# A transformer block with seven-product matmuls: wider weight tiles, x and early h parked in DRAM, and more seven-product chunks

## The chip, the cores and the metric

The kernel runs on one core of one Trainium2 chip. The time is device microseconds of one launch, the median over several runs. The engines in the text are TensorE (PE, with its weight loads as PEld), VectorE (DVE), ScalarE (ACT), GpSimd (POOL) and the queue engine SyncE (SP).

## The reference

One layer on x of 256 x 2048 in float32, batch 1:

```
h    = rms_norm(x, norm_mix);  proj = h @ w_in            # 2048 -> 11264 columns
q_a, f_a, i_a, g_a, q_b, k_b, v_b, gate_logits = split(proj)
gate_a, gate_b = split(sigmoid(gate_logits + b_gate))
y_a  = hgrn2_mixer(q_a, f_a, i_a, g_a)                    # 8 heads of 128, recurrence in chunks
y_b  = chunked_relpos_attention(q_b, k_b, v_b)            # 8 heads of 128
x   += (gate_a * (y_a @ w_proj_a) + gate_b * (y_b @ w_proj_b)) @ w_out
h    = rms_norm(x, norm_ffn)
gate, up = split(h @ w_ffn_in)                            # 2 x 5632 columns
x   += (silu(gate) * up) @ w_ffn_out                      # 5632 -> 2048
```

## The kernel before, in words

All products have 256 rows (two blocks of 128, m = 0 and 1). Weights are cut on the host into blocks of 512 columns and chunks of four k-tiles of 128 rows; one chunk of one block is 1 MB. Each weight is brought by DMA into `raw`, cast to a float32r high half `whi` by ScalarE, and the remainder `wlo` is subtracted out by VectorE. Each product of a 128x128 piece of the activation with a 128x512 piece of a weight is three matmuls, high x high, high x low, low x high (lines 168 to 170, and 222 to 224 in `triple`). Activations are held the same way, as pairs of high and low tiles.

`product` (line 153) computes one block of 512 columns into two PSUM banks: per chunk 4 k-tiles x 2 row blocks x 3 = 24 matmuls. `product_pair` (line 205) computes two blocks at once. In a plain chunk that is 48 matmuls. In a chunk that is listed in `forms`, the first two k-tiles of the chunk, the two row blocks and the two column blocks are treated as a 2 x 2 times 2 x 2 product and done with seven products where eight stand otherwise (`seven`, line 229). That needs four sums of weight tiles (`weight_forms`, line 188) and four sums of activation tiles (`act_forms`, line 318, kept as high and low halves), and eight PSUM banks: four that collect results (`cb`) and four for the shared terms (`ub`), which an epilogue adds up on VectorE after the last such chunk. The other two k-tiles (the "rest" of the chunk) stay plain. With `plain_first`, chunk 0 does its rest first.

The stages in order are: 22 blocks of w_in (with the recurrence and attention woven between the matmuls by generators, which `tick` advances every few products), of which the gate blocks nb = 1 and 3 are pairs in seven form; w_pa and w_pb with the gates; w_out (one pair in seven form, two single blocks); 11 SwiGLU pairs j (the gate block j and the up block 11 + j of w_fi; in seven form for j in `SEVEN_IN`, else two calls of `product`); and w_fo, two pairs of column blocks over 11 chunks, where chunk j reads the 512 columns of h that SwiGLU pair j made; chunks in `SEVEN` are in seven form. The activation forms for these are made when h is transposed (`transpose_split`, line 307, also a generator) and written to DRAM (`kept`), then all read back before w_fo.

Instructions are traced in program order and a planner orders them by priority and by when their inputs and buffers come free in its own model; weight preparation has a priority 500 instructions ahead of its place (`PREP_AHEAD`). An instruction that waits holds up what is behind it on its engine or queue. Raw weight tiles come on SP's queue; `x2_kept`, `kept`, `xt2`, `sf` and `x2` go on POOL's. Tiles come from pools of a fixed number of buffers: `raw` 8 of two 512-column blocks, `whi` and `wlo` 4 of two blocks each, `big` 33 tiles of 4 KB a partition for almost all activations, and two PSUM pools of four banks, `mm` and `aux`.

Of the kernel before, what the change touches and what calls it, by code (L numbers as in the profile page):

```python
# [10 lines left out]
F32 = mybir.dt.float32  # L11
# [6 lines left out]
P = 128  # L18
T = 256
# [17 lines left out]
SEVEN = (1, 2, 3, 5, 6, 7, 9)  # L37


SEVEN_IN = (1, 3, 5, 7, 9)  # L40
# [5 lines left out]
def block_kernel(ctx: ExitStack, tc: tile.TileContext, x, x_t, w_in, w_pa, w_pb, w_out, w_fi, w_fo,  # L46
# [77 lines left out]
    def fetch(w, nb, kc, n=2, pinned=False):  # L124

        res = []
        for hf in range(2):
            raw = wraw_p.tile([P, 2, 512], F32, tag="raw", name=nm("raw"))
            for k in range(0, 2, n):
                d = nc.sync.dma_start(out=raw[:, k:k + n, :],  # L130
                                      in_=w[nb, kc, :, 2 * hf + k:2 * hf + k + n, :])
                if pinned:
                    tc.keep_in_program_order(d)
            res.append(raw)
        return res

    def load_weights(w, nb, kc, n=2, raw=None):

        raw = fetch(w, nb, kc) if raw is None else raw
        res = []  # L140
        for hf in range(2):
            src = raw[hf]
            hi = whi_p.tile([P, 2, 512], F32R, tag="hi", name=nm("whi"))
            lo = wlo_p.tile([P, 2, 512], F32R, tag="lo", name=nm("wlo"))
            for k in range(0, 2, n):
                sl = slice(k, k + n)
                nc.scalar.copy(hi[:, sl, :], src[:, sl, :])  # L147
                nc.vector.tensor_tensor(out=lo[:, sl, :], in0=src[:, sl, :],  # L148
                                        in1=hi[:, sl, :].bitcast(F32), op=ALU.subtract)
            res += [(hi[:, 0, :], lo[:, 0, :]), (hi[:, 1, :], lo[:, 1, :])]  # L150
        return res

    def product(w, nb, n_chunks, act, prologue=None, last=False):

        ps = [mm.tile([P, 512], F32, tag="mm", name=nm("mm")) for _ in range(2)]
        for kc in range(n_chunks):
            if prologue is not None:
                ws = load_weights(w, nb, kc, 1 if kc < 2 else 2, prologue(kc))
            else:
                with tc.high_priority(offset=min(PREP_AHEAD, tc.cur_priority - first_block[0])):  # L160
                    ws = load_weights(w, nb, kc)
# [12 lines left out]
        return ps  # L174
# [5 lines left out]
    def halves(src):  # L180

        n = src.shape[1]
        hi = whi_p.tile([P, 2, 512], F32R, tag="hi", name=nm("whi"))
        lo = wlo_p.tile([P, 2, 512], F32R, tag="lo", name=nm("wlo"))
        split(hi[:, 0:n, :], lo[:, 0:n, :], src)
        return [(hi[:, k, :], lo[:, k, :]) for k in range(n)]

    def weight_forms(r0, r1):


        ta = t6_p.tile([P, 2, 512], F32, tag="t6", name=nm("ta"))
# [12 lines left out]

    def product_pair(w, nbs, n_chunks, act, forms, c_pool, u_pool, epilogue, plain_first=False,
                     last=False):
# [3 lines left out]
        tag = {id(mm): "mm", id(aux): "bank"}  # L210
        cb, ub = {}, {}
        count = [0]
# [16 lines left out]
        def seven(kc, tf):  # L229
            sf = forms[kc]  # L230
            form = {5: 0, 6: 1, 7: 2, 3: 3}
            plain = {1: (0, 0), 2: (1, 0), 4: (1, 1)}
            dest = {2: (0, 0), 3: (0, 1), 4: (1, 0)}
            for p in (1, 2, 3, 5, 7, 6, 4):
                if p in form:
                    a = (sf[:, 0, form[p], :], sf[:, 1, form[p], :])
                else:
                    k, m = plain[p]
                    a = act(kc * 4 + k, m)
                if p in dest:  # L240
                    triple(bank_of(cb, dest[p], c_pool), a, tf[p], False)
                else:
                    triple(bank_of(ub, p, u_pool), a, tf[p], kc == max(forms))
            if kc == max(forms):
                epilogue(ub)

        for kc in range(n_chunks):
            end = kc == n_chunks - 1
            early = plain_first and kc == 0
            with tc.high_priority(offset=min(PREP_AHEAD, tc.cur_priority - first_block[0])):  # L250
                r = [fetch(w, nb, kc) for nb in nbs]
                ws = [[None] * 4 for _ in nbs]
                if kc not in forms:
                    for n in range(2):
                        ws[n][0:2] = halves(r[n][0])
                        ws[n][2:4] = halves(r[n][1])
                else:
                    if not early:
                        tf = weight_forms(r[0][0], r[1][0])
                    for n in range(2):  # L260
                        ws[n][2:4] = halves(r[n][1])
                    if early:
                        tf = weight_forms(r[0][0], r[1][0])
            if kc in forms and not early:
                seven(kc, tf)
# [6 lines left out]
            if kc in forms and early:  # L272
                seven(kc, tf)
# [65 lines left out]

    def picker(tiles):  # L340
# [24 lines left out]
    def x_block(c):  # L365

        xt = t4([P, 4, T], "xt")
        with tc.high_priority():
# [6 lines left out]
            raw = fetch(w_in, 2, c, 1 if c < 2 else 2, pinned=True)  # L375
# [8 lines left out]
        if c == 3:  # L384
            with tc.high_priority():
                for i in range(4):
                    xn = t4([P, 2, 512], "x")
# [367 lines left out]
    def x_forms():  # L755

        for c in range(4):
            xt = t4([P, 2, T], "xt2")
            nc.gpsimd.dma_start(out=xt, in_=x_t[c, :, 0:2, :])
            fq[c] = t4([P, 2, 4, P], "fq", F32R)  # L760
            yield 1
            yield 1
            act_forms(xt, fq[c], par[:, C_NM + 4 * c:C_NM + 4 * c + 4])
# [37 lines left out]
    for nb in range(4):  # L801
# [63 lines left out]
    def swiglu_pair(j):  # L865
# [3 lines left out]
        def sums(ub):  # L869
# [3 lines left out]
        cb = product_pair(w_fi, (j, NJ + j), 4, act_x2, fx, aux, mm, sums, plain_first=True,  # L873
                          last=True)
# [7 lines left out]

    for j in range(NJ):
        if j in SEVEN_IN:
            hn = swiglu_pair(j)
        else:
            ps = product(w_fi, j, 4, act_x2)
# [3 lines left out]
            ps = product(w_fi, NJ + j, 4, act_x2)  # L891
# [7 lines left out]
        soon = dict(wait=0, pool=mm) if j + 1 in SEVEN_IN else {}  # L899
        start(transpose_split(hn, *hT[j], forms=f, spill=spill, **soon))  # L900
# [3 lines left out]
    forms = {}  # L904
    for j in SEVEN:
        forms[j] = t4([P, 2, 4, P], "sf", F32R)
        nc.gpsimd.dma_start(out=forms[j].bitcast(F32), in_=kept[j])
    for pair in range(2):
        nbs = (2 * pair, 2 * pair + 1)
        xs = {nb: t4([P, 2, 512], "x2") for nb in nbs}  # L910
        for nb in nbs:
            nc.gpsimd.dma_start(out=xs[nb], in_=x2_kept[nb])
        x0, x1 = (xs[nb] for nb in nbs)

        pools = (mm, aux) if pair == 0 else (aux, mm)
        cb = product_pair(w_fo, nbs, NJ, act_h, forms, *pools,
                          residual_sums(x0, x1), last=pair == 1)
# [72 lines left out]
```

## Time and profile before

| | us |
|---|---|
| median of 3 runs (lowest, highest) | 1428.51 (1427.79, 1428.94) |
| the profiled execution | 1427.22 |
| its span in the trace | 1425.4 |
| HBM read / written | 279.34 MB / 7.86 MB |

The trace holds one execution. A row of the timeline has the start, the length and the engine of an instruction, its line, its tiles as out<-in, the number of merged instructions, and in brackets how long the engine was idle before it and what ended that. Reported lengths of matmuls overlap their successors, so that what one costs is read from the distance of starts. In a row of a table of stretches, each engine's busy time is followed by its count of instructions; the last three figures are the granted clock of TensorE as a share of full speed, the busy share of the 16 DMA engines, and GB/s.

### The profile page before, as it was taken

Reading aid. Unit: us, or ns where it says so; the run is one execution under the profiler, and the core shown is the slowest. Engines: PE = TensorE matmul, PEld = TensorE weight load, DVE = VectorE, ACT = ScalarE, POOL = GpSimd, SP = SyncE. Lnnn points to the kernel's source line nnn. Section 1 sums busy time; section 2 is a strip of 40 time slices with the busy share of each in tenths; the row PEclk is TensorE's granted clock in tenths of the full one; section 3 lists DMA queues with packets and bytes.
Section 4 is the critical chain, followed back from the end, with each engine's and each line's share of the span. In section 5 each row is a group of like instructions: output and inputs, shape, how many; then the busy total and the mean of one; then the engine's idle time right before and its main releaser. Section 6 shows DMA issues by size and latency. Waiting matters only on the chain.

```text
span 1425.4 us, 17596 instructions
## 1 busy us (share of the span) xinstructions
PE 1417.6 (99%) x6448; PEld 1174.4 (82%) x6448; DVE 1063.6 (75%) x1361; ACT 774.2 (54%) x1009; POOL 50.1 (4%) x63
## 2 busy tenths in 40 slices
PE   9999999999999999999999999999999999999998
PEld 7888888888888888878888888888788888888887
DVE  6768869564878697689767769687796876777875
ACT  7756565555655454455555546455454554544553
POOL 0100100100000000100000000000000010000000
PEclk9999999999999999999999999999999999999999
DMA  9654354446657556547654657656476578666652
GB/s 360 243 192 161 134 193 156 164 163 195 222 183 240 197 197 210 184 148 239 220 203 168 228 169 240 206 179 228 164 238 206 178 254 303 210 221 221 208 183 84
DMA packets 81848, 288.37 MB, mean 202 GB/s; under 512 B 9185, under 2 KB 9441, under 8 KB 81761
## 3 DMA queue, kind: packets, MB, share of 16 engines
q1 hardware_dynamic: 78272, 274.66, 57.5%
q0 software_dynamic: 3488, 12.58, 2.3%
q8 instruction: 50, 0.82, 0.2%
q14 instruction: 38, 0.30, 0.1%
HBM read 279.34 MB, written 7.86 MB: 201 GB/s over the span
## 4 chain that ended last, share of the span: by engine, by line
PE 98%; DVE 1%; ACT 0%; DMA 0%; issue 0%; SPq 0%; DVEq 0%; ACTq 0%
PE mm L169 18%; PE mm L168 18%; PE mm L170 18%; PE mp L223 13%; PE mp L224 13%; PE mp L222 13%; PE bank L285 2%; PE bank L543 1%; DVE wlo L178 1%; ACT whi L177 0%; PE bank L573 0%; DMA raw<-in_w_in 0%; PE bank L619 0%; PE bank L670 0%; PE bank L698 0%; DVE tb L194 0%
## 5 line engine op out<-in xcount | busy, mean ns | idle before, releaser
L148 DVE TENSOR_TENSOR wlo<-raw,whi 128x1024 fp32r<-128x1024 f32 (+1 forms) x292 | 351.9, 1212 | 175.6 <-ACT whi L147 173.4
L147 ACT CAST whi<-raw 128x1024 fp32r<-128x1024 f32 (+1 forms) x292 | 301.9, 1040 | 292.7 <-PE mm L170 219.8
L178 DVE TENSOR_TENSOR wlo<-raw,whi 128x1024 fp32r<-128x1024 f32 x216 | 235.0, 1110 | 51.9 <-ACT whi L177 50.8
L177 ACT CAST whi<-raw 128x1024 fp32r<-128x1024 f32 x216 | 201.2, 960 | 121.8 <-PE mp L224 59.6
L168 PE MATMUL mm<-whi,xTh 128*128 128x512 f32 x576 | 226.6, 398 | 1.3 <-ACT whi L147 1.3
L169 PE MATMUL mm<-wlo,xTh 128*128 128x512 f32 x576 | 225.2, 391 | 0.0
L170 PE MATMUL mm<-whi,xTl 128*128 128x512 f32 x576 | 225.1, 391 | 0.0
L168 PE MATMUL mm<-whi,x2Th 128*128 128x512 f32 x384 | 150.0, 391 | 0.0
L170 PE MATMUL mm<-whi,x2Tl 128*128 128x512 f32 x384 | 149.5, 389 | 0.0
L169 PE MATMUL mm<-wlo,x2Th 128*128 128x512 f32 x384 | 149.4, 389 | 0.0
L168 PEld LDWEIGHTS mm<-whi,xTh 128*128 128x128 f32 x576 | 108.2, 188 | 23.0 <-ACT whi L147 2.0
L170 PEld LDWEIGHTS mm<-whi,xTl 128*128 128x128 f32 x576 | 108.2, 188 | 22.6
L169 PEld LDWEIGHTS mm<-wlo,xTh 128*128 128x128 f32 x576 | 108.3, 188 | 21.8 <-DVE wlo L148 1.0
L223 PE MATMUL mp<-wlo,hTh 128*128 128x512 f32 x282 | 109.7, 389 | 0.0
L224 PE MATMUL mp<-whi,hTl 128*128 128x512 f32 x282 | 109.6, 389 | 0.0
L222 PE MATMUL mp<-whi,hTh 128*128 128x512 f32 x282 | 99.7, 390 | 0.0
L177 ACT CAST whi<-ta 128x1024 fp32r<-128x1024 f32 x46 | 48.3, 1050 | 89.9 <-PE mp L224 87.4
L178 DVE TENSOR_TENSOR wlo<-ta,whi 128x1024 fp32r<-128x1024 f32 x46 | 56.2, 1223 | 48.3 <-ACT whi L177 48.3
L224 PE MATMUL mp<-whi,x2Tl 128*128 128x512 f32 x220 | 86.2, 392 | 0.0
L223 PE MATMUL mp<-wlo,x2Th 128*128 128x512 f32 x220 | 86.2, 392 | 0.0
L170 PEld LDWEIGHTS mm<-whi,x2Tl 128*128 128x128 f32 x384 | 72.1, 188 | 15.0
L168 PEld LDWEIGHTS mm<-whi,x2Th 128*128 128x128 f32 x384 | 72.1, 188 | 14.8
(256 smaller groups left out, 2260.8 us busy)
## 6 DMA issues: line engine op xcount, KB each, us to landing
raw<-in_w_fi SPq DMA_DIRECT2D x176, 512.0 KB, 4.4
raw<-in_w_in SPq DMA_DIRECT2D x172, 512.0 KB, 4.1
raw<-in_w_fo SPq DMA_DIRECT2D x88, 512.0 KB, 5.3
raw<-in_w_out SPq DMA_DIRECT2D x32, 512.0 KB, 4.3
raw<-in_w_pa SPq DMA_DIRECT2D x16, 512.0 KB, 3.7
raw<-in_w_pb SPq DMA_DIRECT2D x16, 512.0 KB, 4.3
x<-x POOLq DMA_DIRECT2D x8, 512.0 KB, 5.7
kept<-sform POOLq DMA_DIRECT2D x7, 512.0 KB, 4.9
```

Of the source, the lines that this page charges most:

```text
L147: nc.scalar.copy(hi[:, sl, :], src[:, sl, :])
L148: nc.vector.tensor_tensor(out=lo[:, sl, :], in0=src[:, sl, :], in1=hi[:, sl, :].bitcast(F32), op=ALU.subtract)
L168: nc.tensor.matmul(ps[m], lhsT=ah, rhs=wh, start=kc == 0 and k4 == 0, stop=False)
L169: nc.tensor.matmul(ps[m], lhsT=ah, rhs=wl, start=False, stop=False)
L170: nc.tensor.matmul(ps[m], lhsT=al, rhs=wh, start=False, stop=kc == n_chunks - 1 and k4 == 3)
L177: nc.scalar.copy(hi, src)
L178: nc.vector.tensor_tensor(out=lo, in0=src, in1=hi.bitcast(F32), op=ALU.subtract)
L222: nc.tensor.matmul(ps, lhsT=ah, rhs=wh, start=first, stop=False)
L223: nc.tensor.matmul(ps, lhsT=ah, rhs=wl, start=False, stop=False)
L224: nc.tensor.matmul(ps, lhsT=al, rhs=wh, start=False, stop=final)
L285: nc.tensor.transpose(out=pt[:, j, m * P:(m + 1) * P], in_=nat[:, m, c:c + P], identity=ident)
L543: nc.tensor.matmul(pl[:, j, :], lhsT=ek[:, g // 2, (g % 2) * P:(g % 2 + 1) * P], rhs=eq[:, g, :], start=True, stop=True)
```

## The change

The weight tiles `raw`, `whi` and `wlo` become four blocks wide (4, 3 and 3 buffers), one cast and one subtraction doing a whole tile; in a pair, a tile holds the same two k-tiles of both column blocks. `big` shrinks from 33 to 25 tiles. x is read for the first norm, dropped, and read again at w_pb; the forms of x and of h come back from DRAM one by one through a pool of three buffers when their chunk is prepared (`form_loader`, on SP's queue), in w_fo once for each of the two pairs; h of pairs 0 to 3 is written to DRAM after its transposes and read back during w_fo's first pair. SwiGLU has seven pairs in seven form instead of five, and the two groups of PSUM banks change roles from one j to the next; between two neighbouring such pairs, the transposes of the first start after the epilogue sums of the second. w_fo takes its chunks in the order 4 to 10, 0 to 3, with nine of eleven in seven form instead of seven.

```diff
-SEVEN = (1, 2, 3, 5, 6, 7, 9)
-SEVEN_IN = (1, 3, 5, 7, 9)
+ORDER = (4, 5, 6, 7, 8, 9, 10, 0, 1, 2, 3)
+SEVEN = ORDER[1:10]
+AWAY = (0, 1, 2, 3)
+SEVEN_IN = (1, 2, 4, 5, 7, 8, 10)
...
-    wraw_p = ctx.enter_context(tc.tile_pool(name="wraw", bufs=8))
-    whi_p = ctx.enter_context(tc.tile_pool(name="whi", bufs=4))
-    wlo_p = ctx.enter_context(tc.tile_pool(name="wlo", bufs=4))
-    big = ctx.enter_context(tc.tile_pool(name="big", bufs=33))
+    wraw_p = ctx.enter_context(tc.tile_pool(name="wraw", bufs=4))
+    whi_p = ctx.enter_context(tc.tile_pool(name="whi", bufs=3))
+    wlo_p = ctx.enter_context(tc.tile_pool(name="wlo", bufs=3))
+    big = ctx.enter_context(tc.tile_pool(name="big", bufs=25))
+    form_p = ctx.enter_context(tc.tile_pool(name="form", bufs=3))
...
+    def fetch(w, parts, n=2, pinned=False):
+        raw = wraw_p.tile([P, 4, 512], F32, tag="raw", name=nm("raw"))
+        for i, (nb, kc, k0) in enumerate(parts):
+            for k in range(0, 2, n):
+                d = nc.sync.dma_start(out=raw[:, 2 * i + k:2 * i + k + n, :],
+                                      in_=w[nb, kc, :, k0 + k:k0 + k + n, :])
...
+        return raw
...
+    def halves(src, pieces=((0, 4),)):
+        hi = whi_p.tile([P, 4, 512], F32R, tag="hi", name=nm("whi"))
+        lo = wlo_p.tile([P, 4, 512], F32R, tag="lo", name=nm("wlo"))
+        for a, b in pieces:
+            split(hi[:, a:b, :], lo[:, a:b, :], src[:, a:b, :])
+        return [(hi[:, k, :], lo[:, k, :]) for k in range(4)]
...
+    def weight_sums(r):
+        t = t6_p.tile([P, 4, 512], F32, tag="t6", name=nm("ts"))
+        op = lambda out, x, y, o: nc.vector.tensor_tensor(out=out, in0=x, in1=y, op=o)
+        op(t[:, 0:2, :], r[:, 2:4, :], r[:, 0:3:2, :], ALU.subtract)
+        op(t[:, 2, :], t[:, 0, :], r[:, 3, :], ALU.subtract)
+        op(t[:, 3, :], r[:, 1, :], t[:, 2, :], ALU.add)
+        return t
...
+                r, rest = (fetch(w, [(nb, kc, k0) for nb in nbs]) for k0 in (0, 2))
+                if kc in forms:
+                    sf = forms[kc]() if callable(forms[kc]) else forms[kc]
+                    if early:
+                        wr = halves(rest)
+                    ts = weight_sums(r)
+                    p1, p2, _, p3 = halves(r, ((0, 2), (3, 4)))
+                    p5, p7, p6, p4 = halves(ts)
...
+    def form_loader(src):
+        def get():
+            f = form_p.tile([P, 2, 4, P], F32R, tag="form", name=nm("sf"))
+            nc.sync.dma_start(out=f.bitcast(F32), in_=src)
+            return f
+        return get
...
+            kept_x = dram.tile([P, 2, 4, P], F32, tag=f"fq{c}", name=nm("fq"))
+            nc.gpsimd.dma_start(out=kept_x, in_=f.bitcast(F32))
+            fq[c] = form_loader(kept_x)
...
+        xs[nb] = t4([P, 2, 512], "x")
+        tc.keep_in_program_order(
+            nc.gpsimd.dma_start(out=xs[nb], in_=x_v[:, :, nb * 512:(nb + 1) * 512]))
...
+            for g in then:
+                start(g)
+        cb = product_pair(w_fi, (j, NJ + j), 4, act_x2, fx, c_pool, u_pool, sums,
+                          plain_first=True, last=True)
...
+    def put_away(j, g):
+        yield from g
+        away[j] = [dram.tile([P, 4, T], F32, tag=f"h{j}_{i}", name=nm("h")) for i in range(2)]
+        for d, src in zip(away[j], hT[j]):
+            nc.gpsimd.dma_start(out=d, in_=src.bitcast(F32))
+    pools = (mm, aux)
+    then = []
     for j in range(NJ):
+        here, other = pools[j % 2], pools[1 - j % 2]
         if j in SEVEN_IN:
-            hn = swiglu_pair(j)
+            hn = swiglu_pair(j, here, other, then)
+            then = []
...
-        soon = dict(wait=0, pool=mm) if j + 1 in SEVEN_IN else {}
-        start(transpose_split(hn, *hT[j], forms=f, spill=spill, **soon))
+        seven_next = j + 1 in SEVEN_IN or j + 1 == NJ
+        late = j in SEVEN_IN and j + 1 in SEVEN_IN
+        g = transpose_split(hn, *hT[j], forms=f, spill=spill, wait=0 if seven_next else 2,
+                            pool=here)
+        g = put_away(j, g) if j in AWAY else g
+        if late:
+            then.append(g)
+        else:
+            start(g)
...
-    for j in SEVEN:
-        forms[j] = t4([P, 2, 4, P], "sf", F32R)
-        nc.gpsimd.dma_start(out=forms[j].bitcast(F32), in_=kept[j])
+    def again(nbs, xs, js):
+        for _ in range(6):
+            yield 1
+        for j in js:
+            hT[j] = split_tiles("hT")
+            for d, dst in zip(away[j], hT[j]):
+                tc.keep_in_program_order(nc.gpsimd.dma_start(out=dst.bitcast(F32), in_=d))
+        for nb in nbs:
+            xs[nb] = t4([P, 2, 512], "x2")
+            tc.keep_in_program_order(nc.gpsimd.dma_start(out=xs[nb], in_=x2_kept[nb]))
     for pair in range(2):
...
+        start(again(nbs, xs, AWAY if pair == 0 else ()))
+        forms = {j: form_loader(kept[j]) for j in SEVEN}
+        cb = product_pair(w_fo, nbs, NJ, act_h, forms, pools[1 - pair], pools[pair],
+                          residual_sums(xs, nbs), last=pair == 1, chunks=ORDER)
```

## Rows read from the trace of the kernel before

**Rows 1.** The page's busy table: time, share of the span, instructions.
```profile
PE 1417.6 (99%) x6448; PEld 1174.4 (82%) x6448; DVE 1063.6 (75%) x1361; ACT 774.2 (54%) x1009; POOL 50.1 (4%) x63
```

**Rows 2.** TensorE's waits, whole span: us in total, times, longest.
```profile
PE mm L168 <- ACT whi L147: 1.3, 1, 1.3
...
PE mp L222 <- ACT whi L177: 1.1, 2, 0.5
```

**Rows 3.** Timeline of TensorE: start, length, engine, line, tiles, count.
```profile
632.20 0.40 PE L224 MATMUL mp<-whi,mTl 128*128 128x512 f32 x1
...
639.59 0.50 PE L222 MATMUL mp<-whi,fm 128*128 128x512 f32 x1
...
812.75 0.40 PE L169 MATMUL mm<-wlo,x2Th 128*128 128x512 f32 x1
...
825.00 0.39 PE L169 MATMUL mm<-wlo,x2Th 128*128 128x512 f32 x1
...
843.13 0.39 PE L222 MATMUL mp<-whi,x2Th 128*128 128x512 f32 x1
```

**Rows 4.** Chain of waits in order of time: start, length, what.
```profile
767.49 0.68 PE mp L222 x3
...
811.11 0.87 PE bank L285 x8
...
856.03 1.06 ACT whi L177
...
941.15 0.68 PE mp L222 x3
...
1114.77 0.68 PE mp L222 x3
```

**Rows 5.** Timeline of DVE and ACT at the start of j=3.
```profile
848.39 0.69 DVE L194 TENSOR_TENSOR ta<-raw,raw 128x512 f32<-128x512 f32 x1
...
849.00 0.68 DVE L194 TENSOR_TENSOR ta<-raw 128x512 f32<-128x512 f32 x1
...
849.47 1.05 ACT L177 CAST whi<-tb 128x1024 fp32r<-128x1024 f32 x1
...
850.56 1.23 DVE L178 TENSOR_TENSOR wlo<-tb,whi 128x1024 fp32r<-128x1024 f32 x1 [0.26 <-ACT whi L177]
...
851.70 0.68 DVE L295 TENSOR_TENSOR hTl<-bank,hTh 128x512 fp32r<-128x512 f32 x1
```

**Rows 6.** Groups by line and shape, DVE and ACT: busy us, mean ns.
```profile
L178 DVE TENSOR_TENSOR wlo<-raw,whi 128x1024 fp32r<-128x1024 f32 x170 | 204.2, 1221 | 45.3 <-ACT whi L177 44.2 <-DMA raw<-in_w_fi 0.2
...
L178 DVE TENSOR_TENSOR wlo<-raw,whi 128x512 fp32r<-128x512 f32 x46 | 32.3, 702 | 6.6 <-ACT whi L177 6.6
...
L177 ACT CAST whi<-raw 128x1024 fp32r<-128x1024 f32 x170 | 173.5, 1052 | 90.2 <-PE mp L224 41.5 <-PE mm L170 36.6 <-DMA raw<-in_w_fi 5.0
...
L177 ACT CAST whi<-raw 128x512 fp32r<-128x512 f32 x46 | 28.6, 622 | 31.6 <-PE mp L224 18.1 <-PE mm L170 13.3
```

**Rows 7.** Busy time by stretch: j=1, j=3, most of w_fo's first pair.
```profile
760.00:802.00 42.00, 42.00 (x190) 34.59 (x189) 38.20 (x44) 25.28 (x29) 0.00 (x0) 1.00 0.58 196
...
847.00:891.00 44.00, 43.46 (x194) 35.17 (x193) 41.09 (x52) 26.57 (x32) 0.53 (x1) 1.00 0.62 205
...
1204.00:1314.00 110.00, 110.00 (x487) 91.11 (x486) 86.16 (x96) 55.08 (x57) 0.00 (x0) 1.00 0.66 213
```

**Rows 8.** DMA: a busy stretch; landing of raw tiles, 1150:1200 and 690:760; forms.
```profile
1180.00:1185.00 5.00, 5.00 (x24) 4.14 (x23) 2.45 (x2) 1.85 (x2) 1.08 (x2) 1.00 1.02 416
...
DMA to landing us min/median/max: 4.4/5.8/8.9
...
DMA to landing us min/median/max: 3.5/3.9/5.1
...
sf<-kept POOLq DMA_DIRECT2D x7, 512.0 KB, 10.1
```

More of the change, by code (lines that the diff above doesn't have):

```diff
@@ L132, in fetch @@
                 if pinned:
                     tc.keep_in_program_order(d)
[L134 to L151, printed above, removed]
@@ L153, in product, with fetch_chunk @@
-    def product(w, nb, n_chunks, act, prologue=None, last=False):
-        ps = [mm.tile([P, 512], F32, tag="mm", name=nm("mm")) for _ in range(2)]
+        return raw
+    def fetch_chunk(w, nb, kc, n=2, pinned=False):
+        return fetch(w, [(nb, kc, 0), (nb, kc, 2)], n, pinned)
+    def halves(src, pieces=((0, 4),)):
[4 more added lines that the diff above has]
+        return [(hi[:, k, :], lo[:, k, :]) for k in range(4)]
@@ L156, in product @@
+    tag = {id(mm): "mm", id(aux): "bank"}
+    def product(w, nb, n_chunks, act, prologue=None, last=False, pool=mm):
+        ps = [pool.tile([P, 512], F32, tag=tag[id(pool)], name=nm("mm")) for _ in range(2)]
         for kc in range(n_chunks):
             if prologue is not None:
-                ws = load_weights(w, nb, kc, 1 if kc < 2 else 2, prologue(kc))
+                n = 1 if kc < 2 else 2
+                ws = halves(prologue(kc), [(k, k + n) for k in range(0, 4, n)])
             else:
@@ L227, in triple, with seven @@
                 tick()
-        def seven(kc, tf):
-            sf = forms[kc]
+        def seven(kc, tf, sf):
             form = {5: 0, 6: 1, 7: 2, 3: 3}
@@ L242, in seven @@
                 else:
-                    triple(bank_of(ub, p, u_pool), a, tf[p], kc == max(forms))
-            if kc == max(forms):
+                    triple(bank_of(ub, p, u_pool), a, tf[p], [kc] == last_form)
+            if [kc] == last_form:
                 epilogue(ub)
-        for kc in range(n_chunks):
-            end = kc == n_chunks - 1
+        for kc in chunks:
+            end = kc == chunks[-1]
             early = plain_first and kc == 0
             with tc.high_priority(offset=min(PREP_AHEAD, tc.cur_priority - first_block[0])):
[L251 to L256, printed above, removed]
-                else:
[L258 to L263, printed above, removed]
+                r, rest = (fetch(w, [(nb, kc, k0) for nb in nbs]) for k0 in (0, 2))
[6 more added lines that the diff above has]
+                    p5, p7, p6, p4 = halves(ts)
+                    tf = {1: p1, 2: p2, 3: p3, 4: p4, 5: p5, 6: p6, 7: p7}
+                    if not early:
+                        wr = halves(rest)
+                    ws = [[None, None, *wr[0:2]], [None, None, *wr[2:4]]]
+                else:
+                    wa, wb = halves(r), halves(rest)
+                    ws = [[*wa[0:2], *wb[0:2]], [*wa[2:4], *wb[2:4]]]
             if kc in forms and not early:
-                seven(kc, tf)
+                seven(kc, tf, sf)
             ks = [k for k in range(4) if ws[0][k] is not None]
@@ L374, in x_block @@
                     tc.keep_in_program_order(nc.sync.dma_start(out=par, in_=params))
-            raw = fetch(w_in, 2, c, 1 if c < 2 else 2, pinned=True)
+            raw = fetch_chunk(w_in, 2, c, 1 if c < 2 else 2, pinned=True)
         hi, lo = split_tiles("xT")
@@ L890, in block_kernel @@
                 nc.scalar.activation(hn[:, m, :], ps[m], AF.Silu, scale=r2[:, m:m + 1])
-            ps = product(w_fi, NJ + j, 4, act_x2)
+            ps = product(w_fi, NJ + j, 4, act_x2, pool=here)
             for m in range(2):
```

65 lines of the change are left out of this document (18 added, 47 removed).

## The prediction

> **What bounds the kernel now.** I read the busy table first [rows 1]: TensorE matmul covers 99% of the span, VectorE 75%. Busy PE says little alone, so the list of TensorE's waits comes next [rows 2]: the longest lines are 1.3 and 1.1 us, on casts of weight tiles, so next to nothing stands between the matmuls. [...]
>
> What could still be won besides matmuls is small. In the chain of waits [rows 4] the same point of pairs j=1, 5 and 9 lies at 767.49, 941.15 and 1114.77: four pairs take 173.6 us. Two plain and two seven-product pairs hold 2 x 192 + 2 x 180 = 744 matmuls, 168.7 us, and 4 x 8 transposes, eight in 0.87 us, 3.5 us: 172.2. So about 1.4 us is lost per four pairs, and the chain shows where: between 849 and 857 it leaves TensorE and runs through casts and subtractions, at the start of j=3 (the second distance is the same, so I charge j=7 alike). Both follow a plain pair that is in SEVEN, so VectorE has activation forms to make just as the seven-product chunks want weights. The third place is the start of w_out: 26 matmuls between 632.20 and 639.59 [rows 3] take 7.39 us where 5.90 would do, 1.5 lost. Together 4.3 us can at most be recovered there.
>
> **The change, part by part.**
>
> *Fewer matmuls.* A chunk in seven form has 7 + 8 products of 3 matmuls, 45 instead of 48. SwiGLU goes from five to seven such pairs of four chunks: 2 x 4 x 3 = 24 fewer. w_fo goes from 7 to 9 such chunks in each of two pairs: 2 x 2 x 3 = 12 fewer. 36 x 0.2268 = **8.2 us less**, on the engine that sets the end. Transposes keep their number.
> [...]
>
> *VectorE, which must feed them.* Reported lengths of neighbours overlap: a 512-wide operation is followed after 0.61 us (848.39 to 849.00), a 1024-wide after 1.14 (850.56 to 851.70) [rows 5]; the step per 512 columns is 0.53, so a 2048-wide takes 1.14 + 2 x 0.53 = 2.2, and 2.3 reported (from 1.22 and 0.70 [rows 6]). A seven chunk before: five 1024-wide and five 512-wide operations, 8.75 us. After: sums 1.14 + 2 x 0.61, the plain factors 1.14 + 0.61, two 2048-wide subtractions 4.4: **8.5 us**, against 45 x 0.2268 = 10.2 of TensorE. Around a seven pair come eight adds (4.9), two products with r2 (1.3), two transposed remainders (1.2) and the forms (1.4): 4 x 8.5 + 8.8 = 43 us, where TensorE has 180 x 0.2268 + 0.9 = 41.7. A plain pair needs 8 x 2.2 + 3.9 = 21.6 of 44.4. A group plain, seven, seven (the new SEVEN_IN repeats that) is 107.6 of 127.8 us, so it fits only if work is done ahead or put off. Ahead: the ring is three tiles of four blocks, 12 blocks, of which a seven chunk uses 11, a whole chunk; before it was eight blocks, two thirds of one. Put off: the transposes between neighbouring seven pairs wait for the end of the second (then), 2.6 us. Inside the two pairs that leaves 86 - 2.6 less the first chunk's 6 us made ahead, 77 of 83 us: 93%. The old seven pairs ran at 38.2 of 42 (91%) without a stall, and 41.1 of 44 with one [rows 7]. Nearest row: no more than the old losses. Bounds for all these starts together: 0 to 3 x 1.4 (j=1, 7, 10 now follow a plain pair of SEVEN, j=4 doesn't) plus 3 x 1 at j=2, 5, 8, so 0 to 7.2 us, where the old kernel had 2.8. I take 3.5: **+0.7**.
>
> *Wider tiles.* One tile is now released, cast and subtracted as a whole. The worst is the "rest" tile: its buffer comes free 24 matmuls before the same place one chunk on, and PE then has 21 matmuls, 4.76 us, and one that needs only the high half, 4.99 in all. Refill: end of the last matmul 0.16 behind its issue step plus 0.04, cast 1.9 (1.05 and 0.62 [rows 6] continued), handoffs of 0.04 [rows 5], subtraction 2.3: 4.5 us. Half a microsecond is left, and 16 of the 24 matmuls do not read the low half. Cost 0 where VectorE is free; up to 0.7 a chunk where a 1024-wide sum (1.22) has just begun. I take **0**, as w_fo has 15% of VectorE free.
>
> *Memory traffic.* w_fo now reads forms twice (18 x 0.5 MB on SP's queue instead of 7 on POOL's ahead of the stage), early h (8 x 0.5) and x2 (4 x 0.5) on POOL's. Pair 0 moves 23 + 4.7 + 4.2 + 1 = 33 MB in 501 x 0.2268 = 114 us, 290 GB/s, against 213 before [rows 7]. From 1180 to 1185 the trace moved 416 GB/s, its DMA engines full, with raw tiles landing after 5.8 us at the median and 8.9 at most from 1150 to 1200 (3.9 and 5.1 from 690 to 760), and POOL's forms after 10.1 [rows 8]; no wait of TensorE lies there [rows 2]. A form ahead of raw tiles on SP's queue delays them by its own 0.5 MB, 1.3 us at that rate; they are wanted a whole chunk later. **0**, bounded by the rival below. The write of fq and its reload have the first gate block (44 us) as cover; x's reload has w_proj; POOL has nothing else queued but the next block's add, pinned behind it. The pool of 33 tiles becomes 25 while 4 x, 4 fq, 8 early h and 7 sf leave it; I count 20 to 26 live at w_proj, w_out and j=9, so single waits are possible, each hidden behind 20 us products: 0 to 2, I take **0**.
>
> Sum against the profiled execution, 1427.2 us (span 1425.4 and 1.8 around it): -8.2 + 0.7 = 1419.7. The median of the runs shown is 1.3 above that execution: **1421 us**.
>
> **Rivals.**
>
> *The ring takes the stalls.* Holding a whole chunk, it absorbs the starts of the seven pairs and of w_out: -8.2 - 4.3 = 1416. For: the stall at 849 began with a tile released late (tb, cast only at 849.5 [rows 5], 6.3 us after the pair's first matmul at 843.13 [rows 3]); the buffer that takes its place now comes free with the plain pair's last matmul. Against: VectorE's 93%.
>
> *VectorE takes over (the other side).* The place: the rest tile in 28 seven chunks of SwiGLU and 18 of w_fo. An engine working in order that has just begun a sum when the cast ends makes TensorE wait up to 0.7; it decides from a mean of 8.2 / 46 = 0.18 us a chunk. At half, 0.35, it costs 16 us: 1428.5 - 8.2 + 16 = 1436. For: 43 us of work against 41.7 in a seven pair, and a slack of 0.5 us behind a 4.5 us chain. Against: the old kernel's w_fo, three seven chunks in a row at 86 of 110 us of VectorE [rows 7], shows no wait.
>
> *Part of that.* The same only at j=1, 2, 4, 5, 7, 8, 10, or slot waits, some 0.7 to 1 us each: +5, 1426.
>
> *The traffic is not hidden.* POOL's 5 MB burst in w_fo meets a demand of 257 GB/s (2.6 MB a chunk with its form, every 10.2 us). If POOL took half of 400 GB/s for 25 us, SP would lack 57 GB/s x 25 us = 1.4 MB, 3.5 us of transfer; with no slack in the raw tiles the time is 1424.5, and with as much again at fq and w_out 1428. [Rows 8] are the evidence against.
> [...]
>
> *It doesn't do what it says.* 36 matmuls fewer is fixed in the code; only their length could change, and nothing in the trace ties that to tile width.
>
> **How the numbers follow.** Forecast (1418 to 1424) 0.45; ring absorbs (1414 to 1418) 0.15; part of the VectorE case 0.17; traffic 0.08; VectorE takes over 0.15. About 0.2%, 2.9 us, is what a measurement of this kernel can tell. Faster than 1425.6: 0.45 + 0.15 + half of the 0.25 in the two mild cases, 0.72. Slower than 1431.4: 0.15. Within: 0.13. The range 1414.5 to 1431 leaves out most of the slow rival and little else.
>
> **What would show it.** TensorE's 512-wide matmuls 36 fewer at an unchanged 0.227 us; four-pair distances replaced by groups plain, seven, seven of about 128 us plus what is lost; waits of TensorE still few and at starts of pairs; seven chunks of w_fo at 10.2 us apart in both pairs; 2048-wide subtractions at 2.3 us. It is wrong if TensorE's waits on wlo recur in every chunk, if the raw tiles' landing grows past 9 us with waits in w_fo's first pair, or if a wait of POOL or ACT for a slot reaches TensorE in the gates or w_out.

## The result, and the profile after

The changed kernel takes 1439.0 us, median of 4 runs (1436.77 to 1440.31), beside 1428.15 of the kernel before: a ratio of 1.0072 (95% interval 1.0060 to 1.0084), 11 us slower by the medians where 7 us faster was forecast. It lies outside the forecast's range, 8 us above its upper end. The profiled execution took 1437.86 us, its span is 1436.1.

The page of the kernel after: busy time and instructions, the shares of the chain of waits by engine, the memory traffic, and the raw tiles' DMAs (issues, KB each, median us to landing).

```profile
PE 1415.1 (99%) x6412; PEld 1169.6 (81%) x6412; DVE 1097.3 (76%) x1153; ACT 750.2 (52%) x790; POOL 58.0 (4%) x82
...
HBM read 295.60 MB, written 15.20 MB: 216 GB/s over the span
...
PE 88%; DMA 5%; DVE 4%; ACT 1%; issue 1%; SPq 0%; DVEq 0%; ACTq 0%
...
raw<-in_w_fi SPq DMA_DIRECT2D x176, 512.0 KB, 5.0
...
raw<-in_w_fo SPq DMA_DIRECT2D x88, 512.0 KB, 6.2
```

TensorE has 36 instructions fewer than in [rows 1], as counted. PE still reads 99%, so that line does not show the loss; the chain does: 12% of the span now runs outside TensorE, 5% through DMAs; before it was 2% in all. The same line of the kernel before:

```profile
PE 98%; DVE 1%; ACT 0%; DMA 0%; issue 0%; SPq 0%; DVEq 0%; ACTq 0%
```

Waits of the kernel after, TensorE's and then VectorE's (us in total, times, longest):

```profile
PE mp L209 <- DVE wlo L178: 12.3, 10, 2.8
PE mp L208 <- ACT whi L177: 1.8, 5, 0.5
...
DVE ts L184 <- DMA raw<-in_w_fi: 22.8, 11, 3.4
DVE ts L184 <- DMA raw<-in_w_fo: 12.7, 6, 4.8
```

L209 is the high x low matmul, L184 the sum of weight blocks, L178 the subtraction that makes `wlo`. [Rows 2] had no wait over 1.3 us; here ten waits for `wlo` take 12.3 us. And VectorE stood 35 us at sums whose raw tile of `w_fi` or `w_fo` had not landed.

How much is that in all? The distances between TensorE's starts, less 0.2267 us for a 512-wide matmul (and the like for narrower ones), add up to 28.6 us lost in the kernel after and 10.7 before: 17.9 more. With 8.2 us of matmuls gone that gives +9.7 of the span's +10.7. By place, after against before: the start of the kernel 7.1 against 5.5; w_out (620 to 660 us) 3.8 against 1.5; the starts of the neighbouring seven pairs, at 780 to 820, 920 to 960 and 1060 to 1100, 4.3, 2.5 and 4.0, where before had two losses of 1.3; from 1180 on, the first chunks of w_fo, POOL's loads and the second pair, 5 together.

The chain of waits of the kernel after at the first of these places (start, length, what):

```profile
791.21 6.00 DMA raw<-in_w_fi
...
797.29 0.09 DVE ts L184
797.38 1.05 issue
798.43 2.29 DVE wlo L178
```

And its timeline there (as in [rows 5]), first VectorE, then ScalarE, then TensorE:

```profile
789.00 1.82 DVE L178 TENSOR_TENSOR wlo<-raw,whi 128x1024 fp32r<-128x1024 f32 x2
...
793.54 0.68 DVE L184 TENSOR_TENSOR ts<-raw,ts 128x512 f32<-128x512 f32 x1
797.29 1.23 DVE L184 TENSOR_TENSOR ts<-raw 128x1024 f32<-128x1024 f32 x1 [3.07 <-DMA raw<-in_w_fi]
798.43 2.28 DVE L178 TENSOR_TENSOR wlo<-raw,whi 128x2048 fp32r<-128x2048 f32 x1
...
793.02 1.92 ACT L177 CAST whi<-raw 128x2048 fp32r<-128x2048 f32 x1 [3.72 <-PE mp L210]
...
795.32 0.39 PE L208 MATMUL mp<-whi,x2Th 128*128 128x512 f32 x1
...
797.13 0.39 PE L210 MATMUL mp<-whi,x2Tl 128*128 128x512 f32 x1
797.36 1.29 PE L208 MATMUL mp<-whi,x2Th 128*128 128x512 f32 x5
800.77 0.80 PE L209 MATMUL mp<-wlo,x2Th 128*128 128x512 f32 x1 [2.12 <-DVE wlo L178]
801.36 0.63 PE L210 MATMUL mp<-whi,x2Tl 128*128 128x512 f32 x1
801.79 0.63 PE L208 MATMUL mp<-whi,x2Th 128*128 128x512 f32 x1
```

Read it backwards. TensorE stands until 800.77 for the low half of the rest tile. Its high half was cast by 794.94. A subtraction begun then would have ended at 797.2, a microsecond before it was wanted (five matmuls from 797.36 need no low half). It began at 798.43, because in VectorE's queue a sum for a later chunk stood ahead of it, and this sum waited 3.07 us for its raw tile. That tile's load could be issued only when the subtractions of 789.00 had freed a buffer (at 790.8), and it landed six microseconds later. The same chain stands at 917 to 932 and 1042 to 1064 us, and at three places from 1184 on (1184, 1232 and 1323), there with landings of 7.4 to 13.5 us. Between 795.32 and 797.13 matmuls still start 0.226 us apart (8 steps in 1.81), so the matmul itself costs what it did in [rows 3]. After the wait they start 0.43 apart: the granted clock of that stretch is 0.66. Two stretches of the kernel after (columns as in [rows 7]):

```profile
800.00:805.00 5.00, 4.23 (x12) 3.37 (x13) 5.00 (x5) 0.00 (x0) 0.00 (x0) 0.66 0.59 209
...
1204.00:1314.00 110.00, 108.70 (x479) 88.58 (x478) 94.56 (x86) 54.65 (x43) 6.36 (x12) 1.00 0.83 305
```

### The profile page after: what moved, and what is told of

Same layout as the page of the kernel before. It is cut to its first block, busy times and chain, and to the rows that moved or that the text cites. A ratio compares the mean times of both kernels' runs of the same rounds, so it can differ in the third digit from the quotient of the medians.

```text
span 1436.1 us, 16750 instructions
## 1 busy us (share of the span) xinstructions
PE 1415.1 (99%) x6412; PEld 1169.6 (81%) x6412; DVE 1097.3 (76%) x1153; ACT 750.2 (52%) x790; POOL 58.0 (4%) x82
## 4 chain that ended last, share of the span: by engine, by line
PE 88%; DMA 5%; DVE 4%; ACT 1%; issue 1%; SPq 0%; DVEq 0%; ACTq 0%
PE mm L168 16%; PE mm L169 16%; PE mm L170 16%; PE mp L209 12%; PE mp L210 12%; PE mp L208 11%; DVE wlo L178 3%; DMA raw<-in_w_fi 2%; DMA raw<-in_w_fo 2%; PE bank L272 2%; ACT whi L177 1%; PE bank L538 1%; DVE ts L184 1%; PE bank L568 0%; DMA raw<-in_w_in 0%
## 5 line engine op out<-in xcount | busy, mean ns | idle before, releaser
L178 DVE TENSOR_TENSOR wlo<-raw,whi 128x2048 fp32r<-128x2048 f32 (+2 forms) x318 | 551.3, 1753 | 205.9 <-ACT whi L177 202.4
L177 ACT CAST whi<-raw 128x2048 fp32r<-128x2048 f32 (+2 forms) x318 | 461.7, 1476 | 414.6 <-PE mp L210 193.6
L177 ACT CAST whi<-ts 128x2048 fp32r<-128x2048 f32 x58 | 110.6, 1907 | 96.7 <-PE mp L210 40.5
L178 DVE TENSOR_TENSOR wlo<-ts,whi 128x2048 fp32r<-128x2048 f32 x58 | 133.3, 2299 | 20.6 <-ACT whi L177 20.6
L209 PE MATMUL mp<-wlo,x2Th 128*128 128x512 f32 x308 | 122.1, 396 | 7.4 <-DVE wlo L178 7.4
L208 PE MATMUL mp<-whi,x2Th 128*128 128x512 f32 x308 | 107.4, 393 | 1.3 <-ACT whi L177 1.3
L184 DVE TENSOR_TENSOR ts<-raw 128x1024 f32<-128x1024 f32 x58 | 70.8, 1221 | 44.8 <-DMA raw<-in_w_fi 22.8
L209 PE MATMUL mp<-wlo,hTh 128*128 128x512 f32 x262 | 102.5, 391 | 2.6 <-DVE wlo L178 2.6
L168 PE MATMUL mm<-whi,x2Th 128*128 128x512 f32 x256 | 99.8, 392 | 0.0
L170 PE MATMUL mm<-whi,x2Tl 128*128 128x512 f32 x256 | 99.4, 390 | 0.0
L209 PEld LDWEIGHTS mp<-wlo,x2Th 128*128 128x128 f32 x308 | 58.3, 189 | 21.5 <-DVE wlo L178 9.9
L208 PEld LDWEIGHTS mp<-whi,x2Th 128*128 128x128 f32 x308 | 58.0, 189 | 14.5 <-ACT whi L177 2.8
```

What stands on the lines that cost most here:

```text
L170: nc.tensor.matmul(ps[m], lhsT=al, rhs=wh, start=False, stop=kc == n_chunks - 1 and k4 == 3)
L177: nc.scalar.copy(hi, src)
L178: nc.vector.tensor_tensor(out=lo, in0=src, in1=hi.bitcast(F32), op=ALU.subtract)
L208: nc.tensor.matmul(ps, lhsT=ah, rhs=wh, start=first, stop=False)
L209: nc.tensor.matmul(ps, lhsT=ah, rhs=wl, start=False, stop=False)
```

## The experiments

Everything here is a variant of the kernel after, run beside the kernel before, whose median in these sets was 1429.0, 1428.6 and 1428.8 us. Two explanations stood against each other: the four-block tiles (the raw ring's four large pieces, or the three large high and low tiles), and the neighbouring seven pairs that load VectorE. Each edit also lets the planner order the instructions anew, so a difference is that of the edit with the order it leads to.

**The old choice of seven chunks, in wide tiles.**

```diff
-SEVEN = ORDER[1:10]
-SEVEN_IN = (1, 2, 4, 5, 7, 8, 10)
+SEVEN = (5, 6, 7, 9, 10, 0, 2)
+SEVEN_IN = (1, 3, 5, 7, 9)
```

> The changed kernel with as many seven-product chunks as the kernel before: SwiGLU pairs 1, 3, 5, 7, 9 and seven chunks of w_fo (at the places in its order where they stood before); everything else as changed. 36 matmuls more than the changed kernel, 8.2 us. Theory A, the wide raw tiles come too late and a sum of weights that waits for one holds up VectorE's queue: every seven stage still loses 1.5 to 4 us at its start, TensorE's waits on low halves stay above 6 us in total, time 1438 to 1446, slower than before. Theory B, VectorE has too much work in neighbouring seven pairs: no neighbours are left, so nearly all the waits go, 1428 to 1433. Theory C, the added DRAM traffic of the parked tensors: it stays, so the waits in w_fo's first pair stay and those of SwiGLU go, 1432 to 1436.

Measured: 1439.34 us (1437.83 to 1440.92), ratio 1.0073 (1.0058 to 1.0088). With no neighbouring pairs and 36 matmuls more it takes as long as the kernel after. That is theory A's time, but not its picture of a loss at every seven stage. The losses moved: only 0.7 and 0.8 us at two pair starts of SwiGLU, but 3.8 at w_out and 9 in w_fo (1300 to 1340 us), where a sum waited 6.35 us for its raw tile (at 1329.89) with the rest's subtraction behind it. TensorE's waits:

```profile
PE mp L209 <- DVE wlo L178: 9.8, 7, 5.7
```

So the wide tiles lose time without any neighbours. In SwiGLU, though, the neighbours count: without them 1.5 us is lost where the three neighbouring starts had cost 10.8.

**All weight tiles two blocks wide again**, with the same bytes: 8 raw, 6 high, 6 low, and the sums `ta` and `tb` as before the change, which also puts the casts of the plain factors ahead of the sums again.

```diff
-    wraw_p = ctx.enter_context(tc.tile_pool(name="wraw", bufs=4))
-    whi_p = ctx.enter_context(tc.tile_pool(name="whi", bufs=3))
-    wlo_p = ctx.enter_context(tc.tile_pool(name="wlo", bufs=3))
+    wraw_p = ctx.enter_context(tc.tile_pool(name="wraw", bufs=8))
+    whi_p = ctx.enter_context(tc.tile_pool(name="whi", bufs=6))
+    wlo_p = ctx.enter_context(tc.tile_pool(name="wlo", bufs=6))
...
-        raw = wraw_p.tile([P, 4, 512], F32, tag="raw", name=nm("raw"))
...
+            raw = wraw_p.tile([P, 2, 512], F32, tag="raw", name=nm("raw"))
...
-        hi = whi_p.tile([P, 4, 512], F32R, tag="hi", name=nm("whi"))
-        lo = wlo_p.tile([P, 4, 512], F32R, tag="lo", name=nm("wlo"))
...
+        hi = whi_p.tile([P, 2, 512], F32R, tag="hi", name=nm("whi"))
+        lo = wlo_p.tile([P, 2, 512], F32R, tag="lo", name=nm("wlo"))
```

> The changed kernel with weight tiles two blocks wide, as before, in the same bytes (raw 8, high and low 6 each): seven pairs, order, DRAM parking and bank groups as changed. Theory A: raw buffers come free in smaller pieces and earlier, sums are four 512-wide operations that each need less, so the waits at the starts go, 1417 to 1423, faster than before. Theory B: VectorE has 0.2 us more to do per chunk, no better, 1437 to 1443. Theory C: traffic is the same, 1435 to 1441.

Measured: **1416.23 us** (1415.82 to 1416.65), ratio 0.9912 (0.9897 to 0.9926), the best of all. Its list of TensorE's waits is complete with two lines, both in the first microseconds:

```profile
PE mm L173 <- ACT whi L182: 1.9, 1, 1.9
PE warm_ps L99 <- DVE warm L96: 1.2, 1, 1.2
```

The width of the tiles, with the order that goes with it, is worth 22.8 us (1439.0 - 1416.2), more than everything else in the change. And VectorE carries the neighbouring pairs without a wait, although it is nearly full (pair 1, pair 2, most of w_fo's first pair):

```profile
760.00:802.00 42.00, 42.00 (x191) 34.74 (x190) 40.63 (x53) 25.13 (x31) 1.65 (x3) 1.00 0.73 237
804.00:848.00 44.00, 44.00 (x200) 36.43 (x199) 41.47 (x52) 25.69 (x31) 1.07 (x2) 1.00 0.66 221
1204.00:1314.00 110.00, 110.00 (x487) 91.06 (x486) 96.83 (x112) 60.80 (x65) 6.92 (x13) 1.00 0.88 320
```

**A sum may not overtake the rest tile.** In wide tiles, the first sum is ordered behind the subtraction of the rest tile before last.

```diff
+BEHIND = 2
...
+        first = op(t[:, 0:2, :], r[:, 2:4, :], r[:, 0:3:2, :], ALU.subtract)
+        tc.add_manual_dep(first.ins, rests[-BEHIND].ins.name,
+                          mybir.DependencyInfo(mybir.DependencyClass.NoSync,
+                                               mybir.DependencyReason.DATA), reason="pin")
```

> The changed kernel with one ordering edge more on VectorE: the first sum of weights of a chunk is issued behind the rest subtraction of the chunk two before it. No tile, load or operation differs. Theory A (the queue's head is the harm): TensorE's waits on low halves fall from 12 us to under 5, 1424 to 1432. If instead the late raw tile itself is what TensorE misses, whatever the order, the waits only move: 1436 to 1442. Theory B: the same work, 1437 to 1441.

Measured: 1431.53 us (1429.77 to 1433.76), ratio 1.0017 (1.0007 to 1.0027). The long waits are gone, short ones remain:

```profile
PE mp L217 <- DVE wlo L181: 5.8, 12, 0.8
PE mp L216 <- ACT whi L180: 2.7, 7, 0.5
```

The order at the head of VectorE's queue is 7.5 us of the 22.8, not all. And at the starts of the neighbouring pairs, where the chain was read, it hardly pays: by the distances of starts they still lose 2.6, 3.3 and 3.5 us. The subtraction now begins at 794.15, as soon as its high half is cast, but from 796 to 820 VectorE is busy without a gap (24.00 of 24 us), and TensorE waits three times, up to 0.73 us, between 811 and 819. Most of the gain lies at w_out and from 1180 on. That points to VectorE's load, the second explanation, as having a share at these starts in wide tiles.

**One raw tile more** (to fit, the forms' pool went from 3 to 2 and `big` to 24).

```diff
-    wraw_p = ctx.enter_context(tc.tile_pool(name="wraw", bufs=4))
+    wraw_p = ctx.enter_context(tc.tile_pool(name="wraw", bufs=5))
...
-    big = ctx.enter_context(tc.tile_pool(name="big", bufs=25))
-    form_p = ctx.enter_context(tc.tile_pool(name="form", bufs=3))
+    big = ctx.enter_context(tc.tile_pool(name="big", bufs=24))
+    form_p = ctx.enter_context(tc.tile_pool(name="form", bufs=2))
```

> The changed kernel with five raw tiles of four blocks instead of four; the forms pool gets two buffers instead of three and the big pool 24 instead of 25, for the room. Theory A: a raw tile is loaded half a chunk earlier (5 us, about its landing of 5 to 6 us), so most of the waits of sums on raw tiles go, 1422 to 1431. Theory B: no gain, 1437 to 1442. Theory C: the loads only start earlier, little gain, 1434 to 1440.

Measured: 1433.47 us (1432.28 to 1437.94), ratio 1.0035 (1.0020 to 1.0049): 5.5 us back, less than theory A said. In its profile the three neighbouring starts lose about 0, 0 and 2 us where they lost 10.8 together, but w_fo from 1345 on, where nothing was lost, loses 6.8. Whether the two form buffers cause that is not shown, so 5.5 us is not the price of the fifth raw tile alone.

**Which of the tiles?** First only `raw` two blocks wide (8), the high and low tiles wide as after. The sums then are four 512-wide operations, and a high and a low tile is filled from two raw tiles, by two 1024-wide casts and two subtractions; only the tiles of sums are still cast and subtracted 2048 wide.

```diff
-    wraw_p = ctx.enter_context(tc.tile_pool(name="wraw", bufs=4))
...
+    wraw_p = ctx.enter_context(tc.tile_pool(name="wraw", bufs=8))
...
+            raw = wraw_p.tile([P, 2, 512], F32, tag="raw", name=nm("raw"))
...
+    def halves(srcs, n=2):
+        hi, lo = wide()
+        for i, src in enumerate(srcs):
+            for k in range(0, 2, n):
+                sl = slice(2 * i + k, 2 * i + k + n)
+                split(hi[:, sl, :], lo[:, sl, :], src[:, k:k + n, :])
```

> The changed kernel with only the raw tiles two blocks wide (8 buffers, same bytes); high and low tiles stay four blocks wide, the sums of a chunk's weights are four 512-wide operations. Theory A1, it is the raw ring's coarse release (a load waits for the subtraction that frees a whole 1 MB tile, then takes 5 to 7 us): most of the gain of the narrow version comes back, 1416 to 1423. Theory A2, it is the coarse release of the high and low tiles: little changes, 1434 to 1440. Both: in between, about 1428.

Then the reverse: `raw` wide, high and low tiles two blocks wide (6 each).

```diff
-    def halves(src, pieces=((0, 4),)):
+    def halves(src, pieces=((0, 2), (2, 4))):
...
+        for h in (0, 2):
+            hi = whi_p.tile([P, 2, 512], F32R, tag="hi", name=nm("whi"))
+            lo = wlo_p.tile([P, 2, 512], F32R, tag="lo", name=nm("wlo"))
```

> The changed kernel with only the high and low tiles two blocks wide (6 buffers each, same bytes); raw tiles and sums stay four blocks wide. Theory A1 (raw ring): the sums still wait on raw tiles, 1432 to 1440. Theory A2 (high and low tiles): 1416 to 1423. Both: about 1428.

Measured: narrow `raw` alone 1445.0 us (1441.45 to 1446.34), ratio 1.0113 (1.0098 to 1.0128), slower still and above every range expected; narrow high and low tiles alone 1420.12 us (1419.35 to 1420.73), ratio 0.9942 (0.9927 to 0.9957). Waits of the first:

```profile
PE mp L227 <- DVE wlo L187: 13.3, 13, 2.0
...
DVE ts L194 <- DMA raw<-in_w_fi: 31.7, 14, 4.5
DVE ts L194 <- DMA raw<-in_w_fo: 24.6, 10, 4.3
```

its subtractions, from raw tiles and from sums:

```profile
L187 DVE TENSOR_TENSOR wlo<-raw,whi 128x1024 fp32r<-128x1024 f32 (+1 forms) x508 | 570.9, 1157 | 142.3 <-ACT whi L186 141.8
...
L187 DVE TENSOR_TENSOR wlo<-ts,whi 128x2048 fp32r<-128x2048 f32 x58 | 133.4, 2299 | 24.0 <-ACT whi L186 23.9
```

and the waits of the second:

```profile
PE mp L214 <- DVE wlo L183: 1.0, 3, 0.4
...
DVE ts L189 <- DMA raw<-in_w_fi: 18.8, 15, 2.8
DVE ts L189 <- DMA raw<-in_w_fo: 17.2, 10, 3.2
```

So a late raw tile does not by itself set the time, though it had looked guilty in the chain: in the second kernel sums wait for raw tiles of `w_fi` and `w_fo` 36 us in all, as long as in the kernel after, and TensorE hardly notices. The raw ring is not cleared by that, for in wide tiles a fifth raw tile took most of the loss off the neighbouring starts. The second kernel's timeline at the place read above, ScalarE, VectorE, then TensorE:

```profile
786.93 1.06 ACT L182 CAST whi<-raw 128x1024 fp32r<-128x1024 f32 x1 [1.40 <-DVE ts L189]
...
790.30 1.22 DVE L183 TENSOR_TENSOR wlo<-raw,whi 128x1024 fp32r<-128x1024 f32 x1
794.33 1.22 DVE L189 TENSOR_TENSOR ts<-raw 128x1024 f32<-128x1024 f32 x1 [2.82 <-DMA raw<-in_w_fi]
795.48 1.22 DVE L183 TENSOR_TENSOR wlo<-raw,whi 128x1024 fp32r<-128x1024 f32 x1
...
796.93 0.84 PE L213 MATMUL mp<-whi,x2Th 128*128 128x512 f32 x3
797.61 0.39 PE L214 MATMUL mp<-wlo,x2Th 128*128 128x512 f32 x1
```

The sum waits 2.82 us here too. But the first half of the same rest tile (790.30) stands ahead of it in VectorE's queue: it was cast at 786.93, where the whole tile's cast began at 793.02, after waiting 3.72 us for TensorE to free its buffer. The second half, from 795.48 to 796.70, is done 0.9 us before TensorE, busy with the first until then, reads it at 797.61. Matmuls there start 0.227 us apart. Why narrow `raw` alone costs 6 us more than none stays open; what shows is that its sums wait longer, 56 us against 35. It also shows that, with narrow `raw`, casting and subtracting the rest tile in two pieces is no cure by itself.

**Wide tiles, cast and subtracted in halves.** The tiles and their release are those of the kernel after; only each long instruction becomes two.

```diff
-    def halves(src, pieces=((0, 4),)):
+    def halves(src, pieces=((0, 2), (2, 4))):
```

> The changed kernel, tiles four blocks wide as changed, but each cast and each subtraction of a whole tile is cut in two 1024-wide instructions (the operations of the version with narrow high and low tiles, in wide buffers). Theory A2a, buffers that come free only four blocks at a time: still 1433 to 1445. Theory A2b, the long instructions (1.9 us cast, 2.3 us subtraction, one after the other): the second half of a cast runs beside the first subtraction, and the time comes down to 1418 to 1424.

Measured: 1425.01 us (1423.39 to 1428.41), ratio 0.9974 (0.9963 to 0.9985), a microsecond above theory A2b's range and far below A2a's. Its busy table and TensorE's wait for `wlo`:

```profile
PE 1409.9 (99%) x6412; PEld 1168.6 (82%) x6412; DVE 1118.4 (79%) x1401; ACT 776.3 (55%) x1040; POOL 61.1 (4%) x82
```

```profile
PE mp L209 <- DVE wlo L178: 3.3, 5, 1.3
```

One line of code gives 14 of the 22.8 us back, although VectorE is busy 21 us longer. Narrow high and low tiles give 4.9 more (1420.1), narrow raw tiles with the old sums on top of these another 3.9 (1416.2). Whether the 14 come from the rest tiles or from the tiles of sums, which the narrow-raw kernel left 2048 wide, no run separates.

**The terms of the sum, in narrow tiles.** The old choice of seven chunks (the edit of the first experiment on the narrow kernel):

> The narrow version (1416.2) with as many seven-product chunks as the kernel before: SwiGLU pairs 1, 3, 5, 7, 9 and seven chunks of w_fo. 36 matmuls more at 0.2268 us: 1424.4 if they are worth their full price on TensorE's path. If neighbouring seven pairs still cost waits, less than that is lost, 1420 to 1423. If the parked tensors cost anything it shows against 1428.5 less the 4.3 us of starts: 1424.2 means they are free.

Measured: 1423.78 us (1423.53 to 1425.92), ratio 0.9968 (0.9959 to 0.9978), with no waits of TensorE but the start's. The 36 matmuls are worth 7.6 us (1423.8 - 1416.2). And against the kernel before, which has the same seven chunks, this kernel with its deeper ring and all the parked tiles' traffic is 4.8 us faster (1428.6 - 1423.8).

The narrow kernel with four high and four low tiles, the ring of the kernel before:

```diff
-    whi_p = ctx.enter_context(tc.tile_pool(name="whi", bufs=6))
-    wlo_p = ctx.enter_context(tc.tile_pool(name="wlo", bufs=6))
+    whi_p = ctx.enter_context(tc.tile_pool(name="whi", bufs=4))
+    wlo_p = ctx.enter_context(tc.tile_pool(name="wlo", bufs=4))
```

> The narrow version with four high and four low buffers instead of six, as in the kernel before (two thirds of a seven chunk ahead instead of a whole one). If the deeper ring is what absorbs the starts of the seven pairs: 1419 to 1424, with TensorE's waits back at starts of pairs. If VectorE's load in neighbouring pairs needs the depth: above 1425. If it is the order of work alone: 1416 to 1417.

Measured: 1431.39 us (1429.53 to 1432.91), ratio 1.0021 (1.0011 to 1.0031). TensorE now waits for casts, at the starts of pairs 1, 2, 4, 5, 7, 8 and 10:

```profile
PE mp L220 <- ACT whi L182: 4.4, 12, 0.6
PE mp L221 <- DVE wlo L183: 1.7, 5, 0.7
```

Eight blocks of ring instead of twelve cost 15.2 us: the neighbouring pairs live on the ring's depth. With the old sevens the deeper ring and the traffic together were worth only those 4.8 us. At eight blocks the change's sevens take longer than the kernel before (1431.4 against 1428.6), in spite of 36 matmuls fewer.

An eighth seven pair, so that four stand in a row (7 to 10):

```diff
-SEVEN_IN = (1, 2, 4, 5, 7, 8, 10)
+SEVEN_IN = (1, 2, 4, 5, 7, 8, 9, 10)
```

> The narrow version (1416.2) with an eighth SwiGLU pair in seven form, j=9, so that 7, 8, 9 and 10 are neighbours: 12 matmuls fewer, 2.7 us. If VectorE's load in neighbouring seven pairs is covered by a ring that holds a chunk: 1413.5. Theory B, four neighbours use up what can be made ahead (43 us of VectorE to 41.7 of TensorE each): waits at 9 and 10 take the gain back, 1416 or more.

Measured: 1419.95 us (1418.7 to 1421.25), ratio 0.9940 (0.9923 to 0.9957): 12 matmuls fewer, 2.7 us by their length, and 3.7 us slower. In the stretch around the added pair VectorE is busy 74.87 of 75 us and TensorE is not:

```profile
1085.00:1160.00 75.00, 73.25 (x325) 59.01 (x324) 74.87 (x101) 44.30 (x54) 1.07 (x2) 1.00 0.60 204
```

There VectorE is the bound, as the forecast feared one step too early. Part of the loss lies behind that stretch: a wait of 2.1 us on VectorE that ends at 1185.

## Why the prediction was wrong

**The step that failed** is *Wider tiles*: "I take **0**, as w_fo has 15% of VectorE free". It measured +22.8 us. The share itself came out (VectorE is busy 94.56 of 110 us there, 14% free), and w_fo lost time all the same. The arithmetic of lengths was good too. The groups of the kernel after that answer to [rows 6]:

```profile
L178 DVE TENSOR_TENSOR wlo<-raw,whi 128x2048 fp32r<-128x2048 f32 x190 | 436.7, 2299 | 192.8 <-ACT whi L177 189.4 <-DMA raw<-in_w_in 3.1
L177 ACT CAST whi<-raw 128x2048 fp32r<-128x2048 f32 x190 | 363.2, 1912 | 345.8 <-PE mp L210 160.3 <-PE mm L170 128.0 <-issue 47.9
```

2.30 and 1.91 us were forecast as 2.3 and 1.9, and the chain of 4.5 us would have met its date at 797.2. What failed is the bound "up to 0.7 a chunk where a 1024-wide sum (1.22) has just begun". It took what can stand ahead on VectorE to be running. In this trace it stood there waiting for a DMA: 3.07 us idle and 1.2 of work. Half a microsecond of slack behind a 4.5 us chain had nothing to meet that with: the subtraction could have begun at 794.94 and began at 798.43, behind the sum. Nor did the free 14% of VectorE keep TensorE from waiting 1.3 us for `wlo` in that stretch of w_fo. The runs show the parts, which overlap: 14 us go when the long casts and subtractions are cut in two, some 9 more when the tiles are; 7.5 go by the order in the queue alone. How the 14 divide between the wait at the head of the queue and the length of the chain stays open.

What "wider" was to save was VectorE's time, and it saved a little: in the narrow-halves kernel two 1024-wide subtractions take 2.27 us from start to start (783.95 to 786.22), in the kernel after one of 2048 takes 2.20 (791.34 to 793.54), and 248 of these make 17 us of VectorE. That was not the bound: with wide tiles and every long instruction cut in two, VectorE is busy 21 us longer and the kernel is 14 us faster.

**Fewer matmuls**, -8.2: right; 7.6 measured, at an unchanged 0.226 us each. The 0.2268 us of the forecast's sum is read from [rows 3]: the 55 matmuls that start from 812.75 to 825.00 us in the kernel before make 54 steps in 12.25 us, at a granted clock of 1.00.

**VectorE, which must feed them**, +0.7: right in the direction that it can, too high in size for narrow tiles. There no wait is left at any pair start, with VectorE at 97% and 94% in the two pairs where 93% was worked out. The limit is one pair further. In wide tiles the three neighbouring starts lost 10.8 us, above the 7.2 that bounded this term, but there it cannot be told apart from the price of the wide tiles.

**Memory traffic**, 0: right where the tiles are narrow (the old sevens with all the traffic gain 4.8 us). In the kernel after, the landing of a raw tile grew to 13.5 us while POOL issued its loads (1226 to 1240), past the 9 us named as a sign; TensorE lost about 2 us there. In the narrow kernel the DMA engines were busier over w_fo's first pair, 0.88 at 320 GB/s against 0.83 at 305 (1204 to 1314), and TensorE did not wait.

**The rivals.** *VectorE takes over*, 1436 at a chance of 0.15, named the place, the rest tile behind a sum in VectorE's queue, and came within 3 us. It was wrong on the form: not 0.35 us in each of 46 chunks but ten waits of up to 2.8, the longest because the sum itself waited; that the times agree is in part luck. *The ring takes the stalls*, 1416, is what the change does once its tiles are narrow: 1416.2. The runs in a row, each term the difference of two of them: 1428.6, -4.8 ring and traffic, -7.6 matmuls, +22.8 wide tiles, 1439.0.

## What to carry to other kernels

Before merging instructions or tiles, list what the longest one stands behind in its engine's queue, and whether that may be waiting for a transfer: here a sum's wait of 3.07 us and its 1.2 us of work held the subtraction until 798.43, 3.5 us after its high half was cast, and w_fo lost time with 14% of VectorE free. Instructions and buffers can be merged apart from each other: with the same twelve blocks of high and low tiles, cutting the instructions in two gave 14 us and cutting the tiles 4.9 more. The last DMA in a chain of waits is not yet the cause: finer raw pieces alone made it worse (1445.0 us against 1439.0), one raw tile more helped some (1433.5), and shorter instructions and finer tiles behind the DMA (1420.1) left its waits about as they were, 36 us against 35, and took most of TensorE's away, 1.0 us for `wlo` against 12.3. And a cure has to be tried at the place where the chain was read: the order of the queue, which looked like all of it there, moved most of that loss to other waits.

## What the runs showed of the hardware

One TensorE wait cost more than itself. It lasted 2.12 us, and from 800.77 us matmuls started 0.43 us apart, near twice the 0.227 before it: the granted clock of 801 to 804 was 0.50, and of 805 to 810 it was 1.00 again. The eight steps to 804.22 took 3.45 us where 1.81 would do, so 1.6 us went on top of the wait. Not every wait does this: after the longest, 2.76 us up to 1064.55, matmuls started 0.33 and then 0.23 us apart, and the granted clock of 1064 to 1069 was 1.00.

Raw tiles of `w_fo` landed after 6.2 us at the median of the kernel after; the eight issued from 1226 to 1245, while POOL's twelve DMA issues (1226.1 to 1240.7) ran beside SP's, landed after 8.4 to 17.0, 12.6 at the median, at 361 GB/s over that stretch.
